# A decoder step on one core: the order of page-row gathers, key products and row sums, with the front and the end of the program rearranged

## The chip, the cores and the metric

The kernel runs as one program on one core of one Trainium2 chip. The metric is device time in microseconds (us), the median of several executions. The engines are TensorE (PE in the profile, with PEld for its weight loads), VectorE (DVE), ScalarE (ACT), GpSimd (POOL, called Pool below) and SyncE (SP). Each engine carries out its own list of instructions in order, and waits at an instruction for semaphores of other engines and of transfers. Transfers are issued by SP, ACT and Pool; the ones that gather cache rows by an index are issued by Pool.

## The reference

One step of a decoder layer for 256 new prompt tokens and for 8 samples of one token each, which have 1024 cached tokens behind them:

```python
xn = rmsnorm(x, g_mix)
q, k, v, b_gate, c_gate, h_in = split(xn @ w_in)      # 1024 -> 6 x 512
att = moba_attend(rope(q), k_all, v_all)              # blocks of 256, best 3 past blocks and the own one
conv_y = b_gate * short_conv(c_gate * h_in)           # width 3
hres = x + concat([att, conv_y]) @ w_out
hn = rmsnorm(hres, g_ffn)
ffn = hier_moe(hn)    # 4 groups x 8 experts: best group, its 2 best experts; sum of gate * (silu(h@Wg)*(h@Wu))@Wd
y = rmsnorm(hres + ffn, g_final)
```

The prompt's attention is over its own 256 tokens. For the samples, k_all and v_all are rows of a paged cache, found through page_table. Outputs are y, the new k and v rows and the new convolution state. All is float32.

## The kernel before

The program is one stretch without loops; two hundred named steps are written as Python functions, and the string `ORDER` (from line 36) lists the names in the order in which they are emitted. Each engine's list of instructions is what the steps give it in that order, so a step's place in ORDER moves it on every engine that it uses.

**Front.** `keep_warm(12)` gives TensorE products without use; then come the norm of the first 128 tokens (`norm1_stats`, `norm1_rs`, `norm1_scale`), a transpose of the norm weights (`pr`) and `pidx` (line 309), a small product that makes the 16 columns of cache row numbers from page numbers. Its input `pgt_` is cast by Pool (line 303), once the page table and a row table have landed. `norm1_T(0)` transposes the normed tokens for the projections (tiles `pt`, `xnT`). The step `pidx` casts the row numbers to integers on VectorE (tile `idx`, line 324). The step `n2` norms and transposes the 8 sample tokens, `q0a` and `q0b` are the two halves of the first query projection (8 matrix products of 128x512 between them), `st1` the norm sums of the second 128 tokens.

**Cache.** `G0` to `G15` gather key tiles (128x2048, 1 MB each: 4 rows of all heads in each partition, two tiles for a sample), `G16` to `G31` value tiles of the same size. They take slots of a ring of nine, so a gather waits until the tile that had the slot before has been used. `Q0` to `Q7` spread a sample's query over 128 partitions (tile `qb` in PSUM). `P0` to `P15` multiply a key tile by that query, in place: tiles 2, 3, 6, 7, 8, 10, 12, 13, 15 on Pool (the list `POOLK`, with ScalarE first copying the query to tile `qv`), the other seven on VectorE. `S0` to `S15` sum each product over the 64 elements of a head (tile `Sd`, on VectorE). When all are done, the steps `self`, `pg` and on choose the blocks and make probabilities; TensorE's first product there is `pself`.

**Prompt attention.** The steps `a0` to `a3` make the scores of two heads each (tile `sc`), add the mask and take the row maximum on VectorE (`pn`, `mx`; line 520 scales the maxima), and the exponentials on ScalarE. `b0` to `b3` and `c0` to `c3` are its products with the values. Between them stand projections (`C..`, `h..`, `B..`), each put off PSUM by ScalarE (`eC..`).

**Values, output, router.** `V0` to `V7` multiply value tiles by the probabilities on TensorE (tile `pov`), `o...` are the output projection (`py`), the rest router and ranking.

**Experts.** Experts are taken in eight groups of four, with 32 slots for each expert: gate products `pgt`, up products `pup` (line 1235), a transposed product `hT`, down products `pyy`, and `pz`, which puts the slots back to tokens with a one-hot matrix. SP issues the weights of all groups in one queue, as slots come free. `slot_maps` and `slot_gates` (lines 1215 and 1204) make the transposed one-hot matrix and each slot's gate with TensorE products (`ppt`, `pgs`).

**End.** The last group's down products are cut into three pieces of the 1024 columns, (0, 512), (512, 768), (768, 1024), so that each can go through `gated` (tile `Y`, a ScalarE and a VectorE part), `combine` (`pz`, or `pzl` for the second and third piece) and `square` (tile `junk`, sums of squares for the last norm) while the next is multiplied. `FIN` are the three token tiles (128, 128 and 8 tokens).

## Time and profile before

| | |
|---|---|
| device time, median of 3 runs | 414.06 us (412.61 to 415.71) |
| the profiled execution's own time | 412.88 us |
| its span | 411.2 us |
| TensorE busy | 371.6 us (90%) |
| VectorE busy | 192.1 us (47%) |
| Pool busy | 103.3 us (25%) |
| ScalarE busy | 98.1 us (24%) |
| transfers | 155.10 MB, mean 377 GB/s |

Times in the profile count from the start of the span. A timeline row gives the start, the time from its first to its last instruction, the engine, the source line, the operation, the tile written and those read, the shape and how many instructions the row holds; in square brackets stands how long the engine was idle before and what it waited for. A row of several instructions spans them. The rows are of the kernel before; after the change, source lines behind line 309 have numbers that are smaller by two in the middle of the file.

### The profile page before, as it was taken

How to read it: one execution, taken by the hardware profiler on the slowest of the kernel's cores; microseconds unless marked ns; L12 is line 12 of the kernel's file. 1: busy time of each engine (PE TensorE's matmuls, PEld its weight loads, DVE VectorE, ACT ScalarE, POOL GpSimd, SP SyncE). 2: the span in 40 equal slices, each digit the busy share in tenths (PEclk: the TensorE clock that was granted, in tenths of full speed). 3: DMA queues.
4: the chain of work that ended last, by engine and by line, in shares of the span. 5: the costliest groups of instructions: out<-in, count | busy, mean ns of one | idle time of the engine just before them, and what ended most of it. 6: DMA issues, size and time to landing. Idle time of an engine off the chain costs nothing.

```text
span 411.2 us, 6610 instructions
## 1 busy us (share of the span) xinstructions
PE 371.6 (90%) x2642; PEld 207.7 (51%) x2642; DVE 192.1 (47%) x381; ACT 98.1 (24%) x244; POOL 103.3 (25%) x102
## 2 busy tenths in 40 slices
PE   5999999999999999999999999995996996999870
PEld 5544436667784534465555555542542552554530
DVE  1248888699883303566644343420420411433153
ACT  4112315244451001142530303020030031030033
POOL 2266978978604300000200000000000000000040
PEclk9899999999999999999999999996996988999996
DMA  7999996977999999999799999999999999999933
GB/s 251 387 405 386 374 379 224 348 282 282 415 410 408 416 419 410 421 415 421 288 420 418 423 420 419 419 422 420 422 421 420 420 420 421 420 419 410 383 124 108
DMA packets 32966, 155.10 MB, mean 377 GB/s; under 512 B 3149, under 2 KB 5435, under 8 KB 18085
## 3 DMA queue, kind: packets, MB, share of 16 engines
q1 hardware_dynamic: 27024, 119.43, 72.4%
q0 software_dynamic: 5136, 33.83, 20.8%
q10 hardware_dynamic: 772, 1.38, 0.9%
q8 instruction: 22, 0.36, 0.4%
q14 instruction: 12, 0.09, 0.1%
HBM read 152.45 MB, written 2.20 MB: 376 GB/s over the span
## 4 chain that ended last, share of the span: by engine, by line
PE 49%; DMA 33%; DVE 10%; issue 3%; POOL 2%; ACT 1%; POOLq 0%; DVEq 0%; ACTq 0%; SPq 0%
DMA g<-in_w_gate_dram 15%; DMA u<-in_w_up_dram 12%; PE py L778 6%; DMA d<-in_w_down_dram 5%; PE pgt L1235 4%; PE pov L723 4%; PE accq L242 4%; PE acck L242 3%; PE accB L560 3%; DVE Sd L487 3%; PE pup L1235 3%; PE pyy L1249 3%; PE pz L1266 3%; PE accv L242 3%; DMA pgt__83<-in_rowtable_dram 2%
## 5 line engine op out<-in xcount | busy, mean ns | idle before, releaser
L1235 PE MATMUL pgt<-g,xg 128*32 128x256 f32 x512 | 40.0, 430 | 12.9 <-DMA g<-in_w_gate_dram 12.5
L1206 POOL TENSOR_TENSOR PGw<-Pg,G 128x384 f32<-128x384 f32 x8 | 6.9, 862 | 162.0 <-PE pgs L1211 89.1
L1300 DVE TENSOR_TENSOR yres<-yres,pz 128x512 f32<-128x512 f32 (+1 forms) x42 | 25.6, 671 | 39.3 <-PE pz L1266 39.3
L481 POOL TENSOR_TENSOR K<-K,qv 128x2048 f32<-128x2048 f32 x9 | 40.7, 4546 | 3.7 <-ACT qv L480 2.5
L487 DVE TENSOR_REDUCE Sd<-K 128x32 f32<-128x2048 f32 x16 | 35.9, 2277 | 4.7 <-POOL K L481 4.7
L1235 PEld LDWEIGHTS pgt<-g,xg 128*32 128x32 f32 x512 | 19.0, 123 | 34.1 <-DMA g<-in_w_gate_dram 18.0
L1249 PE MATMUL pyy<-d,hT 128*32 128x512 f32 (+1 forms) x272 | 34.7, 590 | 0.0
L778 PE MATMUL py<-wo,mixT 128*128 128x512 f32 (+1 forms) x72 | 29.1, 551 | 0.0
L1235 PE MATMUL pup<-u,xg 128*32 128x256 f32 x448 | 27.1, 381 | 0.9 <-DMA u<-in_w_up_dram 0.9
L1075 ACT COPY xr<-px 128x512 f32<-128x512 f32 (+1 forms) x16 | 15.7, 982 | 36.7 <-PE px L1062 36.2
L1258 DVE SCALAR_TENSOR_TENSOR Y<-pyy,gsl,Y 128x512 fp32r<-128x512 f32 (+1 forms) x17 | 12.2, 719 | 25.6 <-ACT Y L1257 25.5
L1330 DVE SCALAR_TENSOR_TENSOR sh<-pup,rsl,sh 128x256 f32<-128x256 f32 x8 | 5.3, 666 | 40.1 <-PE pup L1235 36.3
L1266 PE MATMUL pz<-Y,PT 128*128 128x512 f32 (+1 forms) x90 | 23.6, 406 | 0.3 <-ACT Y L1257 0.2
L1257 ACT ACTIVATE Y<-pyy,gsl 128x512 fp32r<-128x512 f32 (+1 forms) x17 | 11.2, 662 | 44.2 <-PE pyy L1249 25.8
L318 POOL DMA_INDIRECT V<-in_cache_v_dram,idx x16 | 15.1, 947 | 20.9 <-PE pov L723 17.0
L1235 PEld LDWEIGHTS pup<-u,xg 128*32 128x32 f32 x448 | 14.4, 110 | 10.2 <-DMA u<-in_w_up_dram 1.8
L778 PEld LDWEIGHTS py<-wo,mixT 128*128 128x128 f32 x72 | 13.2, 190 | 12.5 <-issue 12.1
L1062 PE MATMUL px<-hn,Pg 128*128 128x512 f32 (+1 forms) x42 | 19.2, 479 | 0.0
L1249 PEld LDWEIGHTS pyy<-d,hT 128*32 128x32 f32 x272 | 9.3, 112 | 19.0 <-issue 13.7
L1266 PEld LDWEIGHTS pz<-Y,PT 128*128 128x128 f32 (+1 forms) x90 | 13.1, 155 | 11.0 <-issue 2.5
L318 POOL DMA_INDIRECT K<-in_cache_k_dram,idx x16 | 15.5, 971 | 10.8 <-DMA K<-in_cache_k_dram,idx 4.8
L483 DVE TENSOR_TENSOR K<-K,qb 128x2048 f32<-128x2048 f32 x7 | 15.9, 2278 | 0.4 <-PE qb L473 0.4
(336 smaller groups left out, 583.6 us busy)
## 6 DMA issues: line engine op xcount, KB each, us to landing
g<-in_w_gate_dram SPq DMA_DIRECT2D x32, 1024.0 KB, 19.7
d<-in_w_down_dram SPq DMA_DIRECT2D x28, 1024.0 KB, 19.9
u<-in_w_up_dram SPq DMA_DIRECT2D x24, 1024.0 KB, 19.8
wo<-in_w_out_dram SPq DMA_DIRECT2D x4, 1024.0 KB, 12.6
uh<-in_w_up_dram SPq DMA_DIRECT2D x8, 512.0 KB, 10.0
u<-in_w_up_dram SPq DMA_DIRECT2D x8, 512.0 KB, 12.0
wk<-in_w_in_dram SPq DMA_DIRECT2D x2, 1024.0 KB
wv<-in_w_in_dram SPq DMA_DIRECT2D x2, 1024.0 KB
```

The lines of the kernel that those rows point to most:

```text
L242: T.matmul(acc, lhsT=xnT[:, cc, 128 * t:128 * t + 128], rhs=W[pn, kk][:, c, :], start=cc == 0, stop=cc == 7)
L318: P.indirect_dma_start(out=t, out_offset=None, in_=src, in_offset=bass.IndirectOffsetOnAxis(ap=idx[:, b, hh:hh + 1], axis=0))
L481: P.tensor_tensor(kslots[i], kslots[i], qv[:, None, :].to_broadcast([128, 4, 512]), op=OP.mult)
L483: V.tensor_tensor(kslots[i], kslots[i], qbs[b][:, None, :].to_broadcast([128, 4, 512]), op=OP.mult)
L487: V.tensor_reduce(Sd[:, b, 4 * hh:4 * hh + 4, :].rearrange("p i h -> p (i h)"), kslots[i].rearrange("p i (h d) -> p (i h) d", h=8), axis=A ...
L723: T.matmul(po[32 * j:32 * j + 32], lhsT=pvs[g][:, b % 4, i, :], rhs=vslots[2 * b + i // 4][:, i % 4, :], start=first and s == 0, stop=left ...
L778: T.matmul(po[:, lo:lo + w], lhsT=mixT[:, c, 128 * t:128 * t + 128], rhs=wo[n, c // 4][:, c % 4, lo:lo + w], start=c == 0, stop=c == 7, sk ...
L1062: T.matmul(PX[grp, hf], lhsT=fl(PgS[grp], t, n), rhs=(hn, hlo)[low][t][:n, 512 * hf:512 * hf + 512], start=t == first and low == 0, stop=t ...
L1235: T.matmul(dst[32 * j:32 * j + 32, 0:256], lhsT=xg[:, c, 32 * j:32 * j + 32], rhs=w[:, 256 * k:256 * k + 256], start=c == 0, stop=c == 7, ...
L1249: T.matmul(py[32 * j:32 * j + 32, 0:w], lhsT=hT[:, c, 32 * j:32 * j + 32], rhs=dw[grp, j][:, 1024 * c + a:1024 * c + b], start=c == 0, sto ...
L1266: T.matmul(pz, lhsT=PTS[grp][:, 128 * t:128 * t + NR[t]], rhs=Y[:, i, 0:w], start=start and i == 0, stop=i == 1, skip_group_check=more)
L1300: V.tensor_tensor(yv, yv, pz[:m], op=OP.add)
```

## The change

The change has four parts.

**Front.** The product `pidx` moves out of the straight code ahead of `norm1_T(0)` into the step `pidx`. The step `n2` is split: `n2s` scales the 8 sample tokens and stands at the front of ORDER, `n2` only transposes them and stands behind `G0 G1`. On TensorE, where `pr` are the transposed norm weights, `pt` transposes and `accq` query products, before:

```order
L306 MATMUL pr<-ident,rows 128x8
L309 MATMUL pidx<-pgt__83 128x16
L224 MATMUL pt<-ident,xn 128x128 x8
L298 MATMUL warm<-ident 128x128 x2
L242 MATMUL accq_206<-wq_97,xnT 128x512 x4
L224 MATMUL pt<-ident,xn 128x8 x8
L242 MATMUL accq_206<-wq_103,xnT 128x512 x4
```

and now:

```order
L306 MATMUL pr<-ident,rows 128x8
L224 MATMUL pt<-ident,xn 128x128 x8
L298 MATMUL warm<-ident 128x128 x2
L242 MATMUL accq_212<-wq_97,xnT 128x512 x4
L323 MATMUL pidx<-pgt__83 128x16
L224 MATMUL pt<-ident,xn 128x8 x8
L242 MATMUL accq_212<-wq_103,xnT 128x512 x4
```

`pidx` has moved from ahead of all transposes to behind the first half of the query products, and the transposes of the 8 sample tokens stay behind it.

**Middle.** In ORDER, gathers stand between Pool's key products, where they were in rows of five before. On Pool, from P6 on (a K or V tile's number is a buffer's; before, K_325, K_360, K_408, K_467 and K_490 are the tiles of P6, P7, P8, P10 and P12), before:

```order
L481 TENSOR_TENSOR K_325<-K_325,qv 128x2048
L481 TENSOR_TENSOR K_360<-K_360,qv 128x2048
L318 DMA K_467<-in_cache_k_dram,idx 128x2048
L318 DMA K_482<-in_cache_k_dram,idx 128x2048
L318 DMA K_490<-in_cache_k_dram,idx 128x2048
L318 DMA K_512<-in_cache_k_dram,idx 128x2048
L318 DMA K_534<-in_cache_k_dram,idx 128x2048
L481 TENSOR_TENSOR K_408<-K_408,qv 128x2048
L481 TENSOR_TENSOR K_467<-K_467,qv 128x2048
L481 TENSOR_TENSOR K_490<-K_490,qv 128x2048
L318 DMA K_556<-in_cache_k_dram,idx 128x2048
```

and now (K_325, K_360, K_408, K_453 and K_468 are the tiles of P6, P7, P8, P10 and P12):

```order
L479 TENSOR_TENSOR K_325<-K_325,qv 128x2048
L316 DMA K_453<-in_cache_k_dram,idx 128x2048
L316 DMA K_455<-in_cache_k_dram,idx 128x2048
L316 DMA K_468<-in_cache_k_dram,idx 128x2048
L479 TENSOR_TENSOR K_360<-K_360,qv 128x2048
L316 DMA K_492<-in_cache_k_dram,idx 128x2048
L479 TENSOR_TENSOR K_408<-K_408,qv 128x2048
L316 DMA K_537<-in_cache_k_dram,idx 128x2048
L479 TENSOR_TENSOR K_453<-K_453,qv 128x2048
L316 DMA K_554<-in_cache_k_dram,idx 128x2048
L316 DMA V_557<-in_cache_v_dram,idx 128x2048
L479 TENSOR_TENSOR K_468<-K_468,qv 128x2048
```

Three gathers stand between P6 and P7, one behind P7, one behind P8, and a key and the first value gather between P10 and P12; the copies of `wr` come behind P12 and a second value gather ahead of P13.

On VectorE, at the same place in the program, the row sum S9 stands ahead of the softmax a1. Before, from the sum S8 on (`mx` are a1's row maxima):

```order
L487 TENSOR_REDUCE Sd<-K_408 128x32
L483 TENSOR_TENSOR K_482<-K_482,qb 128x2048
L512 TENSOR_TENSOR pn<-sc_564,cmask 128x2x128
L512 TENSOR_TENSOR pn<-sc_565,cmask 128x2x128
L518 TENSOR_REDUCE mx<-pn 128x2
L519 TENSOR_REDUCE mx<-pn 128x2
L520 TENSOR_SCALAR mx<-mx 128x4
L487 TENSOR_REDUCE Sd<-K_423 128x32
L487 TENSOR_REDUCE Sd<-K_482 128x32
```

and now:

```order
L485 TENSOR_REDUCE Sd<-K_408 128x32
L481 TENSOR_TENSOR K_455<-K_455,qb 128x2048
L485 TENSOR_REDUCE Sd<-K_423 128x32
L510 TENSOR_TENSOR pn<-sc_567,cmask 128x2x128
L510 TENSOR_TENSOR pn<-sc_568,cmask 128x2x128
L516 TENSOR_REDUCE mx<-pn 128x2
L517 TENSOR_REDUCE mx<-pn 128x2
L518 TENSOR_SCALAR mx<-mx 128x4
L485 TENSOR_REDUCE Sd<-K_453 128x32
```

The sum of K_423 (S9) has moved from behind the maxima to ahead of the masked scores `pn`.

**Last group.** `slot_maps` and `slot_gates` of the last group move from ahead of its gate products to behind them.

**End.** The second piece's down products are no longer emitted in two halves around the first piece's `combine`; all of them follow it, and the third piece's down products follow those. On VectorE, the third piece's `Y` comes ahead of the 8-token square. Before, from the second piece's `Y` on:

```order
L1258 SCALAR_TENSOR_TENSOR Y<-pyy,gsl,Y 128x256
L1395 TENSOR_TENSOR yres<-yres,pz 8x512
L1286 SCALAR_TENSOR_TENSOR junk,ssc<-yres 128x512
L1286 SCALAR_TENSOR_TENSOR junk,ssc<-yres 8x512
L1258 SCALAR_TENSOR_TENSOR Y<-pyy,gsl,Y 128x256
L1406 SCALAR_TENSOR_TENSOR sums<-ssc 128x3
L1414 TENSOR_TENSOR rsc<-ssc,sums 128x3
```

and now:

```order
L1256 SCALAR_TENSOR_TENSOR Y<-pyy,gsl,Y 128x256
L1391 TENSOR_TENSOR yres<-yres,pz 8x512
L1284 SCALAR_TENSOR_TENSOR junk,ssc<-yres 128x512
L1256 SCALAR_TENSOR_TENSOR Y<-pyy,gsl,Y 128x256
L1284 SCALAR_TENSOR_TENSOR junk,ssc<-yres 8x512
L1406 SCALAR_TENSOR_TENSOR sums<-ssc 128x3
L1414 TENSOR_TENSOR rsc<-ssc,sums 128x3
```

The 8-row `junk` and the third `Y` (128x256) have changed places.

The diff:

```diff
--- before.py
+++ after.py
@@ -34,10 +34,10 @@
 KEEP = 6
 POOLK = (2, 3, 6, 7, 8, 10, 12, 13, 15)
 ORDER = """
-wk q0a n2 st1 pidx G0 G1 q0b G2 small2 qs G3 qhl k0a Q0 G4 n1 k0b G5 P0 Q1 q1a S0 P1 G6 k1a P3 P2 Q2 P4 Tq0 q1b S2
-G7 sq P5 Q3 small1 k1b ks G8 mset G9 Tq1 v1a S4 P6 S3 vs P7 v0a v0b S1 S6 G10 Tk1 Tk0 ok G11 S5 C01 G12 a0 G13 C00
-Q4 sk P9 S7 G14 P8 Q6 C11 Q5 P10 P12 S8 G15 P11 v1b a1 wr C03 C02 Q7 eC1 S9 C10 sv S11 P13 G16 eC0 G17 S10
-rs0 rs1 C13 rows2 G18 C12 h00 stT h01 G19 P14 P15 G20 b0 h10 S13 eC2 S12 G21 c0 h02 eC3 S14 eh0 a2 G22 h03 h12
+wk n2s st1 q0a pidx G0 G1 n2 q0b G2 small2 qs G3 qhl k0a Q0 G4 n1 k0b G5 P0 Q1 q1a S0 P1 G6 k1a P3 P2 Q2 P4 Tq0 q1b S2
+G7 sq P5 Q3 small1 k1b ks G8 mset G9 Tq1 v1a S4 P6 S3 vs S1 G10 G11 v0a v0b S6 G12 P7 Tk1 Tk0 ok S5 C01 G13 a0 C00
+Q4 sk P9 S7 P8 G14 Q6 C11 Q5 P10 S8 P11 G15 S9 G16 P12 v1b a1 wr C03 C02 Q7 eC1 C10 sv S10 S11 G17 P13 eC0 G18
+rs0 rs1 C13 rows2 C12 h00 stT h01 P14 G19 P15 G20 b0 h10 S13 eC2 S12 G21 c0 h02 eC3 S14 eh0 a2 G22 h03 h12
 S15 h13 h11 G23 rs2 eh2 G24 B01 D0 self D1 Pp b1 B11 D2 a3 D3 eh1 eh3 B02 D4 rs3 c1 B00 B03 cv3 B12 cv1 cs D5
 cv2 b3 B10 b2 room0 V3 cv0 V0 c2 c3 ov V2 V1 B13 eB1 G25 o010 kvs pe0 o000 eB3 G26 eB0 G27 G28 G29 o110 G30 V5 eB2 V4
 o001 V6 H00 G31 o011 V7 xq H01 l00 pa pe o100 R0 l01 L0 ra0 rb0 rc0 o101 as co ld0 room1 rd0 re0 z0 z1 rk0 oh0 y0
@@ -305,8 +305,6 @@
         pr = ps("pr")
         T.transpose(pr[:, 0:8], rows, ident[0:8, 0:8])
         V.tensor_copy(rowsT[:, 0:8], pr[:, 0:8])
-        pidx = ps("pidx", "qb")
-        T.matmul(pidx[:, 0:16], lhsT=pgt_[:, 0:128], rhs=pgt_[:, 128:144], start=True, stop=True)
         norm1_T(0)
         keep_warm(2)
         idx = small("idx", [128, 8, 2], I32)
@@ -321,6 +319,8 @@
 
         def page_rows():
 
+            pidx = ps("pidx", "qb")
+            T.matmul(pidx[:, 0:16], lhsT=pgt_[:, 0:128], rhs=pgt_[:, 128:144], start=True, stop=True)
             V.tensor_copy(idx.rearrange("p b h -> p (b h)"), pidx[:, 0:16])
 
 
@@ -404,10 +404,8 @@
             V.tensor_copy(rowsT[:, 8:36], pr2[:, 0:28])
 
 
-        @step("n2")
-        def _():
-            norm1_scale(2)
-            norm1_T(2)
+        steps["n2s"] = lambda: norm1_scale(2)
+        steps["n2"] = lambda: norm1_T(2)
 
         @step("st1")
         def _():
@@ -1307,15 +1305,14 @@
                 before(0, "acc")
                 before(1, "acc")
                 before(2, "qb")
-                slot_maps(grp)
-                slot_gates(grp)
             mm_exp(pgt, gw, grp)
             sh = c2("sh", [128, 2, 256])
             sg = sh[:, 0, :]
             S.activation(sg, pgt[:, 0:256], AF.Silu, scale=RSl[grp])
-            if 0 < grp < LAST:
-
-                combine_all(grp - 1, Ys)
+            if grp:
+
+                if grp < LAST:
+                    combine_all(grp - 1, Ys)
                 slot_maps(grp)
                 slot_gates(grp)
             if grp == LAST:
@@ -1385,24 +1382,27 @@
         Y = gated(LAST, pys[0], b0 - a0)
         for t in FIN:
             pz0[t] = ps("pz", ("ms", "qb")[t % 2])[:NR[t]]
-        pys.append(down(LAST, hT, a1, b1, None, (0, 1)))
         combine(LAST, Y, b0 - a0, pz0)
-        down(LAST, hT, a1, b1, pys[1], (2, 3))
-        for t in FIN:
-            if t == 2:
-                Y = gated(LAST, pys[1], b1 - a1)
+        pys.append(down(LAST, hT, a1, b1))
+        pys.append(down(LAST, hT, a2, b2))
+
+        def first_piece(t):
             yv = yres[:NR[t], t, a0:b0]
             V.tensor_tensor(yv, yv, pz0[t], op=OP.add)
             P.tensor_tensor(yo[t][:NR[t], a0:b0], yv, gfin[:NR[t], a0:b0], op=OP.mult)
-        for t in (0, 1):
-            square(0, t, yres[:NR[t], t, a0:b0], V if t == 1 else S)
+
+        first_piece(0)
+        first_piece(1)
+        Y = gated(LAST, pys[1], b1 - a1)
+        first_piece(2)
         combine(LAST, Y, b1 - a1, {t: pzl(1, t) for t in FIN}, False)
-        pys.append(down(LAST, hT, a2, b2))
+        square(0, 0, yres[:NR[0], 0, a0:b0])
+        square(0, 1, yres[:NR[1], 1, a0:b0], V)
+        Y = gated(LAST, pys[2], b2 - a2)
+        combine(LAST, Y, b2 - a2, {t: pzl(2, t) for t in FIN}, False, True)
+        square(0, 2, yres[:NR[2], 2, a0:b0], V)
         for t in FIN:
             square(1, t, pzl(1, t))
-        square(0, 2, yres[:NR[2], 2, a0:b0], V)
-        Y = gated(LAST, pys[2], b2 - a2)
-        combine(LAST, Y, b2 - a2, {t: pzl(2, t) for t in FIN}, False, True)
         V.scalar_tensor_tensor(sums, ssc[:, :, 0], EPS, ssc[:, :, 1], op0=OP.add, op1=OP.add)
         for t in FIN:
             square(2, t, pzl(2, t))
```

## Rows read from the trace of the kernel before

**Rows 1.** The page: the chain by engine, and the gate products' group.

```profile
PE 49%; DMA 33%; DVE 10%; issue 3%; POOL 2%; ACT 1%; POOLq 0%; DVEq 0%; ACTq 0%; SPq 0%
...
L1235 PE MATMUL pgt<-g,xg 128*32 128x256 f32 x512 | 40.0, 430 | 12.9 <-DMA g<-in_w_gate_dram 12.5
```

**Rows 2.** Busy times by stretch: PE, PEld, DVE, ACT, POOL, clock, DMA share, GB/s.

```profile
20.00:36.00 16.00, 16.00 (x57) 7.24 (x56) 8.52 (x20) 3.35 (x6) 9.42 (x12) 1.00 1.03 389
```

**Rows 3.** Timeline (start, us, engine, line, work, idle before): front, PE, then DVE.

```profile
9.87 0.39 PE L309 MATMUL pidx<-pgt__83 10*128 10x16 f32 x2 [2.74 <-POOL pgt__83 L303]
...
17.78 0.16 DVE L324 CAST idx<-pidx 128x16 int32<-128x16 f32 x1
```

**Rows 4.** Timeline of POOL, 25 to 100 us.

```profile
27.32 1.01 POOL L318 DMA_INDIRECT K<-in_cache_k_dram,idx  x1 [1.50 <-DMA K<-in_cache_k_dram,idx]
...
32.56 0.93 POOL L318 DMA_INDIRECT K<-in_cache_k_dram,idx  x1 [1.96 <-DMA K<-in_cache_k_dram,idx]
...
35.86 9.06 POOL L481 TENSOR_TENSOR K<-K,qv 128x2048 f32<-128x2048 f32 x2 [1.13 <-DMA K<-in_cache_k_dram,idx]
...
55.95 9.03 POOL L481 TENSOR_TENSOR K<-K,qv 128x2048 f32<-128x2048 f32 x2
...
65.14 0.98 POOL L318 DMA_INDIRECT K<-in_cache_k_dram,idx  x1 [0.16 <-DVE Sd L487]
...
71.47 13.53 POOL L481 TENSOR_TENSOR K<-K,qv 128x2048 f32<-128x2048 f32 x3 [0.38 <-ACT qv L480]
...
86.28 0.39 POOL L398 COPY wr<-wrt 128x256 f32<-128x256 f32 x1
...
88.83 4.55 POOL L481 TENSOR_TENSOR K<-K,qv 128x2048 f32<-128x2048 f32 x1 [2.15 <-ACT qv L480]
...
97.31 0.94 POOL L318 DMA_INDIRECT V<-in_cache_v_dram,idx  x1 [0.30 <-issue]
```

**Rows 5.** Timeline of DVE, 67 to 95 us.

```profile
67.76 0.17 DVE L520 TENSOR_SCALAR mx<-mx 128x4 f32<-128x4 f32 x1
...
76.03 2.29 DVE L487 TENSOR_REDUCE Sd<-K 128x32 f32<-128x2048 f32 x1 [3.18 <-POOL K L481]
...
80.43 0.75 DVE L512 TENSOR_TENSOR pn<-sc,cmask 128x256 f32<-128x256 f32 x2
...
82.26 2.76 DVE L520 TENSOR_SCALAR mx<-mx 128x4 f32<-128x4 f32 x1
...
94.06 6.66 DVE L487 TENSOR_REDUCE Sd<-K 128x32 f32<-128x2048 f32 x3
```

**Rows 6.** Timeline of ACT at 88 us.

```profile
88.17 0.58 ACT L480 COPY qv<-qb 128x512 f32<-128x512 f32 x1
```

**Rows 7.** Timeline of PE, 109 to 195 us.

```profile
109.25 0.24 PE L649 MATMUL pself<-ones__71,sexp 8*64 8x2 f32 x2 [0.59 <-DVE sexp L646]
...
153.31 1.92 PE L723 MATMUL pov<-V,Pp 128*32 128x512 f32 x16
...
159.18 2.28 PE L723 MATMUL pov<-V,Pp 128*32 128x512 f32 x16
...
194.38 3.66 PE L1235 MATMUL pgt<-g,xg 128*32 128x256 f32 x64
```

**Rows 8.** The tile V: time from issue to landing of its gathers.

```profile
DMA to landing us min/median/max: 5.6/12.7/24.6
```

**Rows 9.** The chain that ended last, near the end (start, us, what).

```profile
374.91 10.23 DMA u<-in_w_up_dram
```

**Rows 10.** Timeline of DVE, 397 to 403 us.

```profile
397.71 0.95 DVE L1286 SCALAR_TENSOR_TENSOR junk<-yres 128x512 f32<-128x512 f32 x1
...
398.60 1.75 DVE L1286 SCALAR_TENSOR_TENSOR junk<-yres 8x512 f32<-8x512 f32 x1
...
400.29 0.47 DVE L1258 SCALAR_TENSOR_TENSOR Y<-pyy,gsl,Y 128x256 fp32r<-128x256 f32 x1
...
402.50 0.16 DVE L1414 TENSOR_TENSOR rsc<-ssc,sums 128x3 f32<-128x3 f32 x1 [1.68 <-ACT junk L1289]
```

## The prediction

> **What bounds the kernel now.** I read the page first. Its chain of work that ended last gives half of the span to TensorE and a third to transfers [rows 1]. The group of the gate products beside it shows where the transfers count: those products wait 12.5 us for gate weights [rows 1]. From the first of them, at 194.38 us [rows 7], weights stream, and the time of that first product is carried to the end one for one. What happens before it is worth what it does to that moment; what happens after the last weights have landed counts by itself.
>
> Next I read the timelines by engine. TensorE has one long wait in front: 2.74 us before pidx, for the page numbers that Pool casts [rows 3]. After that it is busy almost without a gap (16.00 of 16 us between 20 and 36 [rows 2]), but it is not the only chain. Pool and VectorE work through the 16 key tiles, nine products on Pool at 4.5 us each and the sums on VectorE, and TensorE waits 0.59 us at pself (109.25) for the end of that chain [rows 7]. So two chains arrive there nearly together: a gain on TensorE alone is worth nothing past that point, and a loss on the key chain is paid almost in full. Later, at 159.18, 16 value products of TensorE run 2.28 us where 16 took 1.92 at 153.31 [rows 7], which I read as 0.4 us of waiting for values.
>
> **The change, part by part. Front.** pidx goes behind the first query products, so the 2.74 us wait disappears and TensorE runs some 3 us earlier (the 0.39 us of pidx are still paid) [rows 3]. The index cast, at 17.78 now [rows 3], now follows pidx without the third tile's work between them, so cast and gathers come some 3 to 4 us earlier. That brings no key earlier: the transfer engines move 389 GB/s between 20 and 36 us [rows 2], and Pool's waits for landings end at 27.32 and 32.56, two gathers of 1.05 MB in 5.24 us, 400 GB/s, all there is [rows 4]. The same bytes stand ahead of the fourth gather whichever goes first. Pool's first two products wait for that landing (35.86, 1.13 us idle) [rows 4] and stay; so does P6 at 55.95. The 3 us exist on TensorE only, and are lost by pself at the latest.
>
> **Pool's middle.** A gather behind a product takes 0.16 + 0.98 us, each further one 0.30 + 0.94 [rows 4]. After the change P6 ends at 60.5, three gathers follow (to 64.1), and P7 runs 64.1 to 68.6; it began at 60.5 before. The softmax of a0 on VectorE meets this. Its small scaling (TENSOR_SCALAR, 128x4) took 0.17 us at 67.76, with Pool at its gathers; that of a1 took 2.76 us at 82.26 and ended at 85.02, with the end of Pool's three products that began at 71.47 [rows 4, 5]. So that operation waits out a Pool product. For a0 it now waits until 68.6, against an end at 67.9: +0.7. ScalarE's copies for P8 stand behind that softmax, so P8 starts at 72.2 instead of 71.47. It ends at 76.7; then G14; P10 77.9 to 82.4; G15 and G16 (the first value gather); P12 84.8 to 89.3. Before, the three products ran to 85.0.
>
> VectorE meanwhile: sum S8 starts with the end of P8, before at 76.03. S8 and the product behind it take 4.40 us together (76.03 to 80.43), 2.20 each, and from the first row of a1 to its scaling pass 1.83 (80.43 to 82.26) [rows 5]. With S9 put first the scaling arrives 4.40 + 2.20 + 1.83 = 8.43 us after P8, at 85.2. P12 starts 1.16 + 4.51 + 2.40 = 8.07 us after P8, at 84.8. The scaling comes 0.4 us too late and is held until 89.3: +4.3 against 85.0.
>
> The Trainium skill, page "SBUF — State Buffer", section "Who interferes with whom", says that VectorE and GpSimd share one pair of ports as an exclusive lock, that tensor_scalar is among the operations that can take it, that a reduction never does, and that issue order decides who blocks. The row at 82.26 (2.76 us) agrees with that. By that page the forecast is this one, and with the other issue order the first rival below.
>
> Behind the scaling on ScalarE stand a1's exponentials, and behind them the copy of the query for P13, before at 88.17 [rows 6]. It moves to 92.5, so P13 runs 93.1 to 97.65; before it began at 88.83 [rows 4]. VectorE's next three sums began with P13's tile at 94.06 [rows 5]; now they begin at 97.7: +3.6. VectorE's work from there to pself has no gap to give, so pself is 3.6 late, and TensorE with it. Bounds: +1.5 if the scaling is not held (first rival), +4.3 if all of its delay arrives.
>
> **From pself to the first gate product** TensorE's order is unchanged. The 0.4 us at 159 can absorb a part: -0.4 (bounds 0 and -1). The last value gathers wait for TensorE's own value products and move with it.
>
> **Last group.** The transposes and gate sums now follow the gate products. TensorE gains nothing: the second half of the up products waits for weights until 385.1 anyway (the chain's piece from 374.91, 10.23 us [rows 9]). Without that cover the move would still only exchange two pieces of TensorE's work. Zero.
>
> **End.** Uncut, the second piece's products follow pz, and the third's follow at once instead of waiting for pzl. VectorE's Y of the third piece stood behind two squares, the second of which took 1.75 us (398.60), and came at 400.29 [rows 10]. Now it follows the first square (397.71, 0.95 us), at about 398.8; the sum of squares, at 402.50 [rows 10], comes at 401.0. The second square then runs 399.2 to 401.0 and just fits. Gain 1.5 us (bounds 0.5, if that square comes late, and 1.6).
>
> **Sum.** +3.6 - 0.4 - 1.5 = +1.7 us. The durations are of an execution of 412.88 us (span 411.2), 1.2 below the median of 414.06; the difference is put on the median: 415.8 us.
>
> **Rivals.** First: the scaling of a1 is not held. The margin is 0.4 us in 8.4; a wait of G14, G15 or G16 for a free slot would do it. Then a1's scaling ends at 85.4, P12 at 89.3, the copies of wr (the longer 0.39 [rows 4]) and a gather follow, P13 runs 91.0 to 95.6, and the sums behind it start then: +1.5 at pself. 1.5 - 0.4 - 1.5 = -0.4: 413.7 us. For it speaks how thin the margin is, against it that both sides are counted from the same end of P8.
>
> Second: the front's 3 us reach the end of the key chain, because keys do land earlier: the first gathers are served ahead of the projection weights and Pool's first product starts at 32.9. With the scaling free as well: 1.5 - 3.0 - 0.4 - 1.5 = -3.4, 410.7 us. Against it speak the full transfers.
>
> Third, slower: the last values land later. Their margin is gone already at 159.18 [rows 7], the slowest value gather takes 24.6 us [rows 8], and weights fetched in the middle leave the queue in another mix. Each us that the last landing slips beyond TensorE's own 3.6 is one us at the end; from 2.4 us of it the kernel is over 1% slower. With 3 us, 3.6 + 3.0 - 1.5 = +5.1: 419.2 us. Against it: the gathers of the middle are issued earlier, so the bytes ahead of the last ones should rather shrink.
>
> **The numbers.** My forecast 0.50, the first rival 0.22, the second 0.10, the third 0.18. The likeliest gives 415.8 us, its own range 414 to 418. The range for 8 in 10 takes in the first rival and leaves out a part of the second and third: 411.0 to 419.0. One per cent, 4.1 us, is about what a measurement of this kernel can tell from no change. Faster by more (below 409.9) needs the second rival and a further gain at its upper bounds: 0.14. Slower (above 418.2) is the third and the upper end of my forecast: 0.20. Within 1%: 0.66.
>
> **What would show it.** Right: no wait before pt, and pidx behind the query products; Pool's first product still at about 35.9; P7 ending near 68.6; the scaling of a1 lasting several us and ending with P12 near 89; P13 near 93; pself near 113; the first gate product near 197.6; 1.5 us less from the last products to the end. Wrong: a scaling of 0.2 us in a1 (first rival), a Pool product before 34 us (second), TensorE waiting several us for values before 165 us (third).

## The result, and the profile after

The changed kernel takes 416.05 us (median of 20 runs, 415.41 to 417.98), the kernel before 413.97 us beside it (20 runs, 412.38 to 417.81). The ratio is 1.0051, interval 1.0033 to 1.0070: half a per cent slower, 2.1 us. The forecast was 415.8 us, 1.7 us slower.

The profiled execution of the changed kernel took 417.98 us (span 416.2), the longest of its 20, and the one of before 412.88 us, 1.1 below its median. So the two traces lie 5.1 us apart where the medians lie 2.1 apart. What belongs to the change and what to the execution has to be told apart below.

Front, timeline of TensorE after the change:

```profile
7.22 1.06 PE L224 MATMUL pt<-ident,xn 128*128 128x128 f32 x8 [1.33 <-DVE rowsT L307]
...
12.71 0.39 PE L323 MATMUL pidx<-pgt__83 10*128 10x16 f32 x2
```

The wait for the page numbers is gone [rows 3]; pidx stands behind the first half of the query products. Ahead of pt a wait of 1.33 us for a copy of VectorE is left, which the prediction's sign "no wait before pt" did not have. TensorE is 3 to 4 us earlier here.

Pool, 20 to 98 us, after:

```profile
22.27 1.22 POOL L316 DMA_INDIRECT K<-in_cache_k_dram,idx  x1 [1.51 <-DMA K<-in_cache_k_dram,idx]
...
30.35 0.94 POOL L316 DMA_INDIRECT K<-in_cache_k_dram,idx  x1 [3.78 <-DMA K<-in_cache_k_dram,idx]
...
35.55 9.02 POOL L479 TENSOR_TENSOR K<-K,qv 128x2048 f32<-128x2048 f32 x2 [3.01 <-DMA K<-in_cache_k_dram,idx]
...
55.60 4.55 POOL L479 TENSOR_TENSOR K<-K,qv 128x2048 f32<-128x2048 f32 x1
...
63.80 4.57 POOL L479 TENSOR_TENSOR K<-K,qv 128x2048 f32<-128x2048 f32 x1
...
71.94 4.52 POOL L479 TENSOR_TENSOR K<-K,qv 128x2048 f32<-128x2048 f32 x1 [2.44 <-ACT qv L478]
...
84.56 4.53 POOL L479 TENSOR_TENSOR K<-K,qv 128x2048 f32<-128x2048 f32 x1
...
92.93 4.56 POOL L479 TENSOR_TENSOR K<-K,qv 128x2048 f32<-128x2048 f32 x1 [2.20 <-ACT qv L478]
```

The waits of Pool's gathers for landings end at 22.27 and 30.35, where they ended at 27.32 and 32.56 [rows 4]: the first landings come 5 us earlier, later ones 2 us. Pool's first product waits for its keys until 35.55, only 0.3 us earlier than before. P7 begins at 63.80, P8 at 71.94, P12 at 84.56 and P13 at 92.93; the prediction had 64.1, 72.2, 84.8 and 93.1.

VectorE, the scaling of a0 and of a1 and the sums behind P13:

```profile
66.42 1.99 DVE L518 TENSOR_SCALAR mx<-mx 128x4 f32<-128x4 f32 x1
...
84.92 4.20 DVE L518 TENSOR_SCALAR mx<-mx 128x4 f32<-128x4 f32 x1
...
97.52 6.67 DVE L485 TENSOR_REDUCE Sd<-K 128x32 f32<-128x2048 f32 x3 [1.34 <-POOL K L479]
```

"Held" means here that the record of the scaling lasts until the end of a Pool product. The scaling of a0 is held 1.99 us and ends at 68.41, with P7 (68.37), that of a1 4.20 us and ends at 89.12, with P12 (89.09). The sums behind P13 begin at 97.52; the prediction had 97.7, and they stood at 94.06 before [rows 5].

TensorE from 71 us to the first gate product:

```profile
71.92 0.49 PE L471 MATMUL qb<-qhi,selr 128*128 128x512 f32 x1 [3.71 <-ACT qv L478]
...
72.48 5.29 PE L242 MATMUL accv<-wv,xnT 128*128 128x512 f32 x8
...
91.33 2.05 PE L558 MATMUL acch<-xnT,wh 128*128 128x264 f32 x8 [2.21 <-ACT mixT L562]
...
112.72 0.24 PE L647 MATMUL pself<-ones__71,sexp 8*64 8x2 f32 x2 [1.84 <-DVE sexp L644]
...
114.03 3.39 PE L558 MATMUL accB<-xnT,wB 128*128 128x264 f32 x8
...
135.41 3.79 PE L721 MATMUL pov<-V,Pp 128*32 128x512 f32 x32
...
164.49 1.92 PE L721 MATMUL pov<-V,Pp 128*32 128x512 f32 x16
...
199.33 3.66 PE L1233 MATMUL pgt<-g,xg 128*32 128x256 f32 x64
```

The same places before:

```profile
71.44 0.49 PE L473 MATMUL qb<-qhi,selr 128*128 128x512 f32 x1 [0.33 <-ACT qv L480]
...
72.00 3.59 PE L242 MATMUL accv<-wv,xnT 128*128 128x512 f32 x8
...
110.32 1.95 PE L560 MATMUL accB<-xnT,wB 128*128 128x264 f32 x8
...
130.25 3.64 PE L723 MATMUL pov<-V,Pp 128*32 128x512 f32 x32
```

TensorE has three long waits, where the longest of before was 0.59 us at pself: 3.71 us for ScalarE's copy of a query behind the held softmax of a0, 2.21 us for a copy off PSUM behind that of a1, and 1.84 us at pself. With the first of them the front gain is gone (71.92 against 71.44). pself comes at 112.72, 3.47 us later than before [rows 7]. The last value products take 1.92 us, so the 0.4 us of waiting at that place [rows 7] are gone; an earlier group takes 3.79 us where it took 3.64, so 0.2 us are gained on values. The first gate product starts at 199.33, 4.95 us later than before.

So 1.5 us came on top between pself and there: 1.7 us of a lower clock, less the 0.2. Stretches of the changed kernel: us, busy times of PE, PEld, DVE, ACT, POOL, the granted TensorE clock, the DMA share and GB/s:

```profile
74.00:76.00 2.00, 2.00 (x4) 0.88 (x3) 0.00 (x0) 0.00 (x0) 2.00 (x1) 0.50 0.00 0
...
114.00:115.00 1.00, 1.00 (x5) 0.79 (x4) 0.86 (x7) 0.62 (x2) 0.00 (x0) 0.50 1.01 416
```

After the wait of 3.71 us TensorE ran at a granted clock of 0.50 (1.2 GHz), so that the eight accv products at 72.48 took 5.29 us instead of 3.59, and after the wait at pself again, so that eight accB products took 3.39 us instead of 1.95. In the trace of before the clock is 1.00 in both stretches. The first of the two lies ahead of the waits at 91.33 and at pself, which take up what it costs; the second counts. It belongs to this execution: in the profiled executions of the other kernels below the clock behind pself is 1.00, and pself to the first gate product takes 84.8 to 85.8 us (85.1 before, 86.6 here).

The end, on all engines: the first down product, VectorE's third Y and the square that now follows it, ScalarE's first square of the second piece, and the total:

```profile
394.90 2.85 PE L1247 MATMUL pyy<-d,hT 128*32 128x512 f32 x16
...
403.78 0.47 DVE L1256 SCALAR_TENSOR_TENSOR Y<-pyy,gsl,Y 128x256 fp32r<-128x256 f32 x1
...
404.18 1.35 DVE L1284 SCALAR_TENSOR_TENSOR junk<-yres 8x512 f32<-8x512 f32 x1
...
404.73 0.38 ACT L1287 ACTIVATE junk<-pzl 128x256 f32<-128x256 f32 x1 [1.62 <-PE pzl L1264]
...
407.01 0.16 DVE L1414 TENSOR_TENSOR rsc<-ssc,sums 128x3 f32<-128x3 f32 x1 [0.91 <-ACT junk L1287]
```

The third Y comes right behind the first square, as forecast. But ScalarE's squares of the second piece start only at 404.73, behind the third piece's products, and six of them stand in line there. The first down product before:

```profile
389.63 3.61 PE L1249 MATMUL pyy<-d,hT 128*32 128x512 f32 x24
```

From the first down product to the total it is 12.11 us, against 12.87 us before (389.63 to 402.50 [rows 10]): 0.76 us gained.

### The profile page after: what moved, and what is told of

It is laid out like the page before. It is cut to its first block, busy times and chain, and to the rows that moved or that the text cites. A ratio compares the mean times of both kernels' runs of the same rounds, so it can differ in the third digit from the quotient of the medians.

```text
span 416.2 us, 6609 instructions
## 1 busy us (share of the span) xinstructions
PE 369.5 (89%) x2642; PEld 208.5 (50%) x2642; DVE 197.5 (47%) x381; ACT 98.2 (24%) x244; POOL 104.0 (25%) x102
## 5 line engine op out<-in xcount | busy, mean ns | idle before, releaser
L1247 PE MATMUL pyy<-d,hT 128*32 128x512 f32 (+1 forms) x272 | 33.2, 584 | 0.0
L1233 PEld LDWEIGHTS pup<-u,xg 128*32 128x32 f32 x448 | 16.4, 110 | 8.6 <-DMA u<-in_w_up_dram 2.1
L1247 PEld LDWEIGHTS pyy<-d,hT 128*32 128x32 f32 x272 | 8.4, 111 | 18.4 <-issue 15.3
L558 PE MATMUL acch<-xnT,wh 128*128 128x264 f32 x64 | 15.5, 393 | 2.2 <-ACT mixT L562 2.2
```

Of the source, the lines that this page charges most:

```text
L558: T.matmul(acc[:, 0:264], lhsT=W[pn, kk][:, c, 128 * m:128 * m + 128], rhs=xnT[:, cc, 0:264], start=cc == 0, stop=cc == 7)
L1233: T.matmul(dst[32 * j:32 * j + 32, 0:256], lhsT=xg[:, c, 32 * j:32 * j + 32], rhs=w[:, 256 * k:256 * k + 256], start=c == 0, stop=c == 7, ...
L1247: T.matmul(py[32 * j:32 * j + 32, 0:w], lhsT=hT[:, c, 32 * j:32 * j + 32], rhs=dw[grp, j][:, 1024 * c + a:1024 * c + b], start=c == 0, sto ...
```

## The experiments

Three spans carry most of the readings. The first is from Pool's first key product to pself, which takes out that keys land at another time in each execution; the second is from the last group's first down product to the total of squares; both come from one profiled execution of each kernel. The third is the time against the kernel before, run beside it on the same chip: its median there was 414.76 us for x1 to x4, 414.12 for x5 to x8, 414.21 for x9 to x11 and 414.39 for x12. The ratio is the recorded one, with a 95% interval; it can lie some tenths of a per cent from the quotient of the two medians.

| kernel | first Pool product | from there to pself | end | us | ratio to before, interval |
|---|---|---|---|---|---|
| before | 35.86 | 73.39 | 12.87 | 413.97 | 1 |
| the change | 35.55 | 77.17 | 12.11 | 416.05 | 1.0051 (1.0033 to 1.0070) |
| x1_front_end | 35.28 | 73.05 | 12.06 | 412.12 | 0.9938 (0.9910 to 0.9966) |
| x2_middle | 35.50 | 77.12 | 12.79 | 419.30 | 1.0116 (1.0066 to 1.0166) |
| x3_scale_act_after | 35.90 | 73.09 | 12.07 | 412.94 | 0.9943 (0.9915 to 0.9971) |
| x4_scale_act_before | 38.89 | 70.89 | 12.82 | 413.78 | 0.9956 (0.9926 to 0.9987) |
| x5_squares_early | 35.40 | 77.14 | 11.39 | 414.76 | 1.0026 (0.9999 to 1.0052) |
| x6_front | 35.30 | 72.96 | 12.82 | 413.61 | 0.9996 (0.9973 to 1.0020) |
| x7_end | 37.20 | 74.00 | 12.09 | 413.33 | 0.9991 (0.9968 to 1.0013) |
| x8_all | 35.47 | 70.87 | 11.38 | 408.25 | 0.9870 (0.9837 to 0.9904) |
| x9_s9_back | 35.77 | 76.57 | 12.09 | 415.75 | 1.0032 (1.0015 to 1.0049) |
| x10_all_old_front | 37.13 | 70.93 | 11.34 | 409.78 | 0.9894 (0.9865 to 0.9923) |
| x11_all_new_middle | 35.55 | 73.10 | 11.34 | 411.04 | 0.9937 (0.9909 to 0.9964) |
| x12_wr_between | 35.30 | 74.95 | 12.09 | 413.47 | 0.9971 (0.9936 to 1.0006) |

**The change without its middle, and the middle alone.** x1_front_end is the changed kernel with these lines of ORDER as before; x2_middle is the kernel before with the new ones (the beginning of the first line and the end of the third, which stay, are left out):

```diff
-S1 G10 G11 v0a v0b S6 G12 P7 Tk1 Tk0 ok S5 C01 G13 a0 C00
-Q4 sk P9 S7 P8 G14 Q6 C11 Q5 P10 S8 P11 G15 S9 G16 P12 v1b a1 wr C03 C02 Q7 eC1 C10 sv S10 S11 G17 P13 eC0 G18
-rs0 rs1 C13 rows2 C12 h00 stT h01 P14 G19 P15 G20
+P7 v0a v0b S1 S6 G10 Tk1 Tk0 ok G11 S5 C01 G12 a0 G13 C00
+Q4 sk P9 S7 G14 P8 Q6 C11 Q5 P10 P12 S8 G15 P11 v1b a1 wr C03 C02 Q7 eC1 S9 C10 sv S11 P13 G16 eC0 G17 S10
+rs0 rs1 C13 rows2 G18 C12 h00 stT h01 G19 P14 P15 G20
```

> The changed kernel with the middle's order as it was before: new front, new last group and end, old order of gathers, key products and row sums. Theory (the middle costs because the scaling of a1 waits out Pool's P12): the scaling of a0 takes 0.2 us again, pself comes no later than before (109.3), the end's gain of about 0.7 us stays: 412.6 to 413.4 us, that is 0.6 to 1.4 below before. Rival (the early TensorE is itself the harm: it runs ahead in front, then waits, and its clock is halved afterwards): a stretch at half clock near 72 to 76 us stays and the time is 415 to 416 us.

> The kernel before with only the middle's new order of gathers, key products and row sums; front, last group and end as before. Theory: the scaling of a1 is held about 4 us until P12 ends, P13 starts 4 us late, pself 3 to 4 us late: 416.5 to 417.5 us, slower than the whole change, since the end's gain is missing. Rival (the early TensorE is the harm): within 0.5 us of before, 413.5 to 414.5 us.

The scalings of x1_front_end on VectorE:

```profile
66.15 0.17 DVE L518 TENSOR_SCALAR mx<-mx 128x4 f32<-128x4 f32 x1
...
81.34 2.77 DVE L518 TENSOR_SCALAR mx<-mx 128x4 f32<-128x4 f32 x1
```

and that of a1 in x2_middle:

```profile
84.85 4.20 DVE L520 TENSOR_SCALAR mx<-mx 128x4 f32<-128x4 f32 x1
```

With the old middle, a0 is not held, a1 is held 2.77 us as before, pself lies where it lay (73.05 us behind the first Pool product, 73.39 before), and the kernel is 0.6% faster than before. With the new middle alone a1 is held 4.20 us, pself is 3.7 us late as in the whole change, and the kernel is 1.2% slower. So the loss is the middle's. The rival, that the early TensorE does the harm, falls: x2_middle has no early TensorE and is the slowest of all, and x1_front_end has one and keeps a clock of 1.00 from 60 to 125 us. x1_front_end gained more than expected, 2.6 us by the ratio instead of 0.6 to 1.4. The median of x2_middle is above what was expected (416.5 to 417.5); one of its six runs was 416.0, the other five 418.6 to 421.3, and the profiled one is the 416.0, so what the five have more is not seen.

**The scaling taken off VectorE.** One line in the softmax of each head pair, in the changed kernel (x3_scale_act_after) and in the kernel before (x4_scale_act_before):

```diff
-            V.tensor_scalar(mx, mx, -SCALE, None, op0=OP.mult)
+            S.activation(mx, mx, AF.Copy, scale=-SCALE)
```

> The changed kernel with one instruction moved from VectorE to ScalarE in each of a0 to a3: the scaling of the row maxima (128x4), so that it can no longer wait for a Pool product. Theory: a0's exponentials start near 66.7 instead of 68.4, P8 near 69.7 instead of 71.9, a1's exponentials near 83 instead of 89.2, P13 directly behind its gather near 88.5 instead of 92.9, pself near 109: 411.5 to 413 us, 3 to 4.5 below the changed kernel. Rival (the interleaved gathers delay Pool's products, and the held scaling only fills time that is lost anyway): P13 moves by under 1 us and the time stays at 415.5 to 416.5 us.

> The kernel before with the scaling of the row maxima moved from VectorE to ScalarE. Theory: a1's exponentials start near 82.6 instead of 85.1, P13 near 86.8 instead of 88.8, but TensorE is only 0.6 us behind that chain at pself, so little of it counts: 412.8 to 413.6 us. Rival (the held scaling costs the kernel before its full 2.6 us too): 411.2 to 411.8 us.

In x3_scale_act_after, ScalarE's scaling of a1, and P13 on Pool:

```profile
83.48 0.21 ACT L518 ACTIVATE mx<-mx 128x4 f32<-128x4 f32 x1 [0.78 <-DVE mx L517]
```

```profile
89.34 4.56 POOL L479 TENSOR_TENSOR K<-K,qv 128x2048 f32<-128x2048 f32 x1
```

The 128x4 scaling takes 0.21 us on ScalarE and nothing holds it; a1's exponentials follow at once, P13 starts 3.6 us earlier than in the change, and the kernel falls by 1.1 percentage points to 0.9943 of before. This is the experiment on the hold itself: gathers, products and sums stand exactly as in the change, and only the instruction that waits for Pool has left VectorE. The rival as it was put, that P13 moves by under 1 us and the time stays, falls. But the kernel before has a held scaling too, so this does not yet say how much of the loss the new order costs by itself; x4_scale_act_before and x11_all_new_middle do.

In x4_scale_act_before, the first and the seventh Pool product:

```profile
38.89 9.05 POOL L481 TENSOR_TENSOR K<-K,qv 128x2048 f32<-128x2048 f32 x2 [4.72 <-DMA K<-in_cache_k_dram,idx]
...
89.32 4.55 POOL L481 TENSOR_TENSOR K<-K,qv 128x2048 f32<-128x2048 f32 x1
```

P13 comes 50.4 us after the first product, against 53.0 before (88.83 less 35.86 [rows 4]), and pself 2.5 us earlier in the same count. In this profiled execution keys landed 3 us later than in that of before, so its 415.6 us hide the gain; the ratio over all runs shows one (0.9956). Its interval of 0.5 to 3.1 us takes in what was expected as well as the rival's 2.6, so how much of the 2.5 us reaches the end is not decided.

**The end.** x7_end is the kernel before with the new last group and end alone. x5_squares_early is the changed kernel with

```diff
+        for t in FIN:
+            square(1, t, pzl(1, t))
         combine(LAST, Y, b2 - a2, {t: pzl(2, t) for t in FIN}, False, True)
         square(0, 2, yres[:NR[2], 2, a0:b0], V)
-        for t in FIN:
-            square(1, t, pzl(1, t))
```

> The kernel before with only the new last group and end. Theory: the last norm's factors come 0.7 us earlier counted from the last up products, time 0.1 to 0.25% below before. Rival (first working of the prediction): 1.5 us, 0.35 to 0.4% below before.

> The changed kernel with one move in the end: the three sums of squares of the second piece are emitted ahead of the third piece's combine, so that ScalarE need not wait for the third piece's products on the same PSUM tiles. Theory (the end gained 0.7 instead of 1.5 us because ScalarE's six squares stood in line behind the last product): three squares lie behind the last product again, the end is 0.9 to 1.1 us shorter, time 0.2 to 0.3% below the changed kernel, that is 0.2 to 0.3% above before. Rival (the transfer of the last down weights or VectorE's second square bounds the end): no difference from the changed kernel, 0.5% above before.

x5_squares_early, at the end: the first down product, the first square of the second and of the third piece on ScalarE, and the total:

```profile
392.79 2.84 PE L1247 MATMUL pyy<-d,hT 128*32 128x512 f32 x16
...
401.30 0.38 ACT L1287 ACTIVATE junk<-pzl 128x256 f32<-128x256 f32 x1 [0.19 <-PE pzl L1264]
...
402.97 0.38 ACT L1287 ACTIVATE junk<-pzl 128x256 f32<-128x256 f32 x1 [0.50 <-PE pzl L1264]
...
404.18 0.16 DVE L1414 TENSOR_TENSOR rsc<-ssc,sums 128x3 f32<-128x3 f32 x1 [0.51 <-ACT junk L1287]
```

The second piece's squares now start at 401.30, while the third piece is still multiplied, and the end takes 11.39 us. That is 1.48 us less than before, the 1.5 us of the prediction; as the change has it, 0.76 us come. The step is worth 0.72 us, less than the 0.9 to 1.1 expected. In time x5_squares_early is 0.25% below the change. x7_end is too small for its interval (0.9968 to 1.0013); its trace shows about the same, 0.78 us.

**The front.** x6_front is the kernel before with the new place of pidx and the split of n2:

> The kernel before with only the new front (pidx behind the first query products, the 8 sample tokens split off). Theory (the front's 3 us exist on TensorE alone; keys do not land earlier): Pool's first product at 35 to 36 us, pself within 1 us of before, time 0 to 0.25% below before. Rival (gathers that are issued earlier make the landing of the first keys steadier, it is up to 3 us later in some executions of the kernel before): the median falls by 0.4 to 0.6% and the runs lie closer together.

The time is that of before (0.9973 to 1.0020), pself moves from 109.25 to 108.26, and Pool's first product from 35.86 to 35.30. The front's 3 us on TensorE are worth nothing by themselves, as forecast. The median did not fall as the rival had it, and the 12 runs lie 4.4 us apart (411.6 to 416.0; the 29 of before beside them 7.3), so the rival is not supported here; x10_all_old_front below comes back to it.

**All that helped.** x8_all has the new front, the old middle, the scaling on ScalarE, and the new end with the squares early:

> New front and end, the middle's order as before, the scaling of the row maxima on ScalarE, and the second piece's squares ahead of the third combine: all that the runs so far speak for. Theory: against new front and end alone (0.6% below before) the end gives 1.0 us more and the free scaling moves P13 from 87.9 to about 86 and pself by 0.6 to 1.5 us: 409.5 to 411 us, 0.9 to 1.2% below before. Rival (with the early front the key chain is bound by landings only): the scaling gives nothing, 0.8 to 0.9% below before.

Pool's P13, and pself, in x8_all:

```profile
85.89 4.54 POOL L479 TENSOR_TENSOR K<-K,qv 128x2048 f32<-128x2048 f32 x1
```

```profile
106.34 0.24 PE L647 MATMUL pself<-ones__71,sexp 8*64 8x2 f32 x2 [0.27 <-DVE sexp L644]
```

408.25 us (five runs from 408.13 to 408.40), 1.3% below before and 1.8% below the change: more than expected. P13 comes 2.9 us and pself 2.9 us earlier than before [rows 4, 7], and the end is 1.5 us shorter.

Two variants take one part of it back: the old front (x10_all_old_front), and the change's middle (x11_all_new_middle).

> The fastest kernel so far (new front and end, old middle, scaling on ScalarE, squares early) with the front as before. Theory (the front's gain exists on TensorE only and is lost at pself): at most 0.8 us slower than with the new front, 408.3 to 409.2 us. Rival (the new front makes the landing of the first keys steadier; without it Pool's first product comes up to 3 us late in some executions): 409.5 to 411.5 us and runs that lie 3 us apart instead of 0.3.

> The fastest kernel so far with the middle's order as in the change (gathers between Pool's products, S9 first). Theory (once nothing is held, the interleaved gathers still put P12 and P13 later): pself 2 to 2.5 us later than with the old order (109 against 106.3), 410 to 411 us. Rival (the held scaling was all that the new order cost): 408 to 408.6 us, the same as the old order.

x11_all_new_middle is 411.04 us: with nothing held any more, the new order still puts pself 2.2 us later (73.10 against 70.87), with P12 and P13 some 3 us later behind more gathers. The other pair with a free scaling says the same: 73.09 in x3_scale_act_after against 70.89 in x4_scale_act_before. So the new order costs twice. Of its 3.8 us, 2.2 are its own and 1.6 come from the longer hold.

x10_all_old_front is 409.78 us, with runs from 408.57 to 411.19. Pool's first product there:

```profile
37.13 9.06 POOL L481 TENSOR_TENSOR K<-K,qv 128x2048 f32<-128x2048 f32 x2 [2.75 <-DMA K<-in_cache_k_dram,idx]
```

It came at 37.13. Time and spread are those of the rival. In the nine profiled kernels with the new front Pool's first product came between 35.28 and 35.90, in the five with the old front at 35.50, 35.86, 37.13, 37.20 and 38.89. The times lie closer too: of the kernels with ten runs or more, those with the new front spread over 1.1 to 2.6 us and x6_front over 4.4, those with the old front over 3.0 to 7.3. That speaks for the rival, that early gathers make the landing of the first keys steadier; but the intervals of x8_all and x10_all_old_front overlap, and x6_front alone was not faster. It stays open.

**Who comes first.** x9_s9_back puts S9 behind a1 again and the first value gather behind P12; x12_wr_between also puts Pool's two small copies ahead of P12. The part of the line that changes, for x9_s9_back:

```diff
-P10 S8 P11 G15 S9 G16 P12 v1b a1 wr
+P10 S8 P11 G15 P12 v1b a1 S9 G16 wr
```

and for x12_wr_between

```diff
-P10 S8 P11 G15 S9 G16 P12 v1b a1 wr
+P10 S8 P11 G15 wr P12 v1b a1 S9 G16
```

> The changed kernel with the sum S9 behind the softmax a1 again, and the first value gather (which needs S9's slot) behind P12. Nothing else is moved. Theory (who issues first decides): a1's scaling arrives 2.2 us earlier, near 82.7, P12 only starts near 83.3, so the scaling takes 0.2 us; P12 ends near 87.9, P13 starts near 91 behind two gathers, pself 1.5 to 2.5 us earlier than in the changed kernel: 413 to 414.5 us. Rival (the scaling is held by whatever Pool does around it): scaling of 4 to 5 us again and 416 us or more.

> As the run with S9 put back, but Pool's two small copies of wr (0.2 and 0.4 us) stand between the gather G15 and the product P12. In that run a1's scaling came 0.6 us before P12's recorded start, during the gather, and was held all the same. Theory A (while the gather runs, the Pool instruction behind it already has the ports): the scaling that comes at about 83 waits at least for the copies, 0.7 us or more, and perhaps for P12 as well, to 88.7. Theory B (a gather does not hold the scaling, and Pool's product simply started about 0.6 us before its record): with 0.6 us of copies in between the scaling takes 0.2 us, a1's exponentials start near 83.2, and the time is 413.5 to 415 us.

x9_s9_back, Pool's gather and P12, and the scaling of a1:

```profile
82.56 0.97 POOL L316 DMA_INDIRECT K<-in_cache_k_dram,idx  x1 [0.16 <-DVE mx L516]
...
83.55 4.53 POOL L479 TENSOR_TENSOR K<-K,qv 128x2048 f32<-128x2048 f32 x1
```

```profile
82.96 5.15 DVE L518 TENSOR_SCALAR mx<-mx 128x4 f32<-128x4 f32 x1
```

The scaling came 0.59 us ahead of P12 by the records and was held 5.15 us all the same, to P12's end. The theory that whoever starts first in the records wins falls; the time, 415.75 us, is close to the change's. x12_wr_between, the gather, the first of the two copies and P12, and the scaling:

```profile
82.03 0.97 POOL L316 DMA_INDIRECT K<-in_cache_k_dram,idx  x1 [0.16 <-DVE mx L516]
...
83.00 0.23 POOL L397 COPY wr<-wrt 128x32 f32<-128x32 f32 x1
...
83.51 4.54 POOL L479 TENSOR_TENSOR K<-K,qv 128x2048 f32<-128x2048 f32 x1
```

```profile
82.44 0.17 DVE L518 TENSOR_SCALAR mx<-mx 128x4 f32<-128x4 f32 x1
```

With 0.5 us of copies in between, a scaling that comes 0.56 us ahead of the copies and 1.07 us ahead of P12 takes 0.17 us. Both scalings came 0.4 us into a gather, so it is not the gather that holds for microseconds (nor in [rows 5], where 0.17 us at 67.76 fell into one). In x7_end a scaling late in a gather (68.96 to 69.90) took 0.35 us and ended with it:

```profile
69.54 0.35 DVE L520 TENSOR_SCALAR mx<-mx 128x4 f32<-128x4 f32 x1
```

A product, by these two executions, holds from some time between 0.6 and 1.1 us ahead of its recorded start. Whether the product really starts earlier than its record or takes something in advance is not settled. x12_wr_between is also the first rival of the prediction made real: 1.6 us more to pself than before. Its 413.47 us lie near that rival's 413.7, in part by luck, since that sum had 1.5 us for an end that gave 0.8.

## Why the prediction was right, and where it was off

**The middle: right, mechanism and size in the trace.** The prediction had the scaling of a1 held until 89.3 (89.12 measured), P13 from 93.1 (92.93), the sums behind it from 97.7 (97.52) and pself 3.6 us late (3.47; 3.8 counted from the first Pool product). x1_front_end and x2_middle show that the middle holds the whole loss, and x3_scale_act_after that pself comes 4.1 us earlier when the scaling is not held (73.09 against 77.17). The hold is one of two causes: with a free scaling in both orders the new one still costs 2.2 us. The prediction had both, with +1.5 us for the case in which only a1's scaling comes free, and x12_wr_between measured 1.6. The Trainium skill, page "SBUF — State Buffer", section "Who interferes with whom", names tensor_scalar among the operations that can take the ports shared with GpSimd, and an exclusive lock; the 4.20 us that end with P12 agree. Its rule that issue order decides is not borne out in x9_s9_back if issue is read as the recorded start: the scaling's is 0.59 us ahead of the product's and it lost. The moment of issue itself stands in no record.

**The front: right where it counts.** "No key earlier" was too strong: the first landings came 5 us earlier. But the lead had shrunk to 0.3 us at Pool's first product (35.55 against 35.86), and TensorE's gain was lost in a wait at 71.92, before pself.

**Values at 159 us: right, but smaller.** The 0.4 us are gone (1.92 us at 164.49), and 0.15 came at an earlier group, so 0.2 are gained; the last values were no further bound, so the third rival did not happen. That rival's "from 2.4 us of it" should be 2.0 by its own sum, which leaves the 0.4 out.

**The last group: no effect seen.** From the first gate product to the last group's first down product it is 195.25 us before and 195.57 in the change; the other kernels lie between 194.98 and 196.43. It was not run by itself.

**The end: right place, wrong size.** The step "the squares' total comes at 401.0" was 1.5 us and is 0.76. I had counted that VectorE's Y moves ahead of a square, but not that the new code emits the second piece's squares behind the third combine. They read the PSUM tiles which that combine goes on writing, so ScalarE waited for its products, and six squares followed instead of three. x5_squares_early gives the missing 0.7 us.

**The sum: right, perhaps in part by luck.** With the terms as measured, 3.5 - 0.2 - 0.8 = 2.5 us; the medians differ by 2.1. The experiments divide this difference in another way. The middle alone costs 1.16% (x2_middle, 4.8 us, interval 2.7 to 6.9), and front and end together give 0.62% (x1_front_end, 2.6 us, interval 1.4 to 3.7), where the traces show 3.3 and 0.8. The first interval takes in the 3.3, the second does not take in the 0.8. So by the medians the middle and the rest would be off by 1.5 to 2 us each, with opposite signs, and the 2.1 comes out all the same. What front and end have more is not explained: alone they gave 0.04 and 0.09%. Steadier landings would fit, but are not shown.

That the two profiled executions differ by 5.1 us is the half clock behind the wait at pself (1.7 us), and a long execution beside a short one. With it the first gate product came at 199.33, where the prediction had 197.6. The clock was not in the prediction, and what decides it is open: it stayed at 1.00 behind a wait of 2.77 us at the same place in x11_all_new_middle:

```profile
108.65 0.24 PE L647 MATMUL pself<-ones__71,sexp 8*64 8x2 f32 x2 [2.77 <-POOL Pp L635]
```

**The first rival's condition was off.** The prediction had the scaling come 0.4 us behind the start of P12 (0.36 measured: 84.92 against 84.56) and let it go free if P12 came later by that much. x9_s9_back shows that being 0.59 us ahead does not suffice, so P12 would have had to come about 1 us later or more, and the chance of 0.22 was too high. The chance of 0.14 for a time below 409.9 was too high by the prediction's own numbers: it needs the second rival, which had 0.10.

## What to carry to other kernels

Where Pool multiplies large tiles, look for small VectorE operations between its products, in the rows that last microseconds instead of tenths and end with a Pool instruction; move them to ScalarE before the order of anything else is touched. Here that one line was worth 1.1 percentage points on the changed kernel. A gain on one engine in front is worth little if a second chain meets it later (x6_front: 0.9996), so free that chain too: new front and end gave 0.6%, with the scaling moved and the squares early 1.3%. And check a sum that comes out right against its parts: here the medians divide it otherwise than the traces do. And when a piece of an end is moved, read for each engine what the moved writes make its readers wait for.

## What the runs showed of the hardware

- A 128x4 scaling on VectorE took 0.17 us, or up to 5.15 us when a Pool product of 4.5 us held it; on ScalarE it took 0.21 us. Row sums and VectorE's own products of 128x2048 took 2.27 to 2.29 us throughout, beside Pool's products too.
- The hold begins before the product's recorded start: a scaling 0.59 us ahead of it was held, one 1.07 us ahead was not (one execution each). A scaling inside a gather took 0.17 us, and 0.35 in one case that ended with the gather.
- TensorE's granted clock fell from 1.00 to 0.50 behind waits of 3.71 us and 1.84 us, and eight products took 5.29 us instead of 3.59 and 3.39 instead of 1.95. It stayed at 1.00 behind a wait of 2.21 us in the same trace and behind one of 2.77 us in x11_all_new_middle.
- Pool's first product started between 35.28 and 38.89 us in the 14 profiled executions, as its keys landed. These 3.6 us are more than the effect of most edits here.
